# Down projections of an encoder trunk: twelve instead of eight inner chunks by half-block products

## The chip, the cores and the metric

The kernel runs on one core of a Trainium2 chip. The metric is the device time of one execution in microseconds. A core has TensorE (PE in the profile; its weight loads are shown as PEld), VectorE (DVE), ScalarE (ACT), GpSimd (POOL) and SyncE (SP), which run their own instruction queues in order and wait for one another by semaphores. Transfers are issued from the queues of SP and POOL. Matmul results lie in PSUM, everything else in SBUF.

## The reference

The reference is an encoder of two layers on 512 tokens of width 1024 in float32. Each layer has a SwiGLU half step, an attention mixer, a second SwiGLU half step and a gated embedding:

```python
def swiglu(x, w_gate, w_up, w_down):
    return (jax.nn.silu(x @ w_gate) * (x @ w_up)) @ w_down
...
h = h + 0.5 * swiglu(rmsnorm(h, norm_ffn1[i]), ...)
h = h + ab_mixer(...) if i % 2 == 0 else h + c_mixer(...)
h = h + 0.5 * swiglu(rmsnorm(h, norm_ffn2[i]), ...)
h = h + sigmoid(rmsnorm(h, norm_ple[i]) @ w_ple_gate[i]) * (p[i] @ w_ple_proj[i])
```

The inner width is 2816, which is 22 chunks of 128. So there are four down projections, from 22 inner chunks to 8 output chunks of 128 features by 512 tokens.

## The kernel before

Activations lie transposed, features on the partitions and 512 tokens along the row. Float32 accuracy is kept by splitting each operand into a high part (a rounded copy, ScalarE, line 149) and a low part (the difference, VectorE, line 150); a product is three matmuls: high by high, high by low, low by high.

In `ffn` the gate and up projections make the inner chunks one after the other (m = 0 to 21). Each is split into two activation tiles of the pool `act`. The first eight are also stored unsplit to DRAM (`raw`, line 408, from POOL's queue).

`down` (line 418) then makes the output chunks in four pairs. The first pair is plain: for each output 22 chunks of 128, three matmuls of 512 columns each (`plain`, lines 433 to 440), with weights loaded in units of up to eight chunks, and every unit split into a tile of `whi` and one of `wlo` (four buffers each). During that pair `inner_sums` (line 504) fetches the stored chunks k and k + 4 for k = 0 to 3 and makes the combinations that the half-block products need.

For the other three pairs (m = 2, 4, 6), inner chunks 0 to 7 go by seven products instead of eight: two outputs by two groups of four chunks by two halves of the tokens make a two by two block product, and Winograd's form of Strassen's scheme needs seven block products of 256 columns. `inner_weights` (line 521) loads 1024 columns of both outputs and combines them on VectorE (lines 529 to 533), making four weight tiles: wa, wb, ws, wr. The seven products go into PSUM banks p1, p2 (pool `psmm`, three buffers), y (`pss`) and z (`pso`). Then y is copied (lines 482 and 489), combined with z (490 to 492) and added to the residual (494). The remaining 14 chunks of each output are added plainly, into p1 and p2, and `evict` (line 442) adds the bank to the residual, stores the output to `kept` in DRAM and normalises it (`norm_chunk`: lines 199 and 200 make the split, 207 the square, 214 the running sum of squares on POOL). Outputs in LATER (3, 4, 5) are not normalised then; they are fetched back behind the seven products of the last pair (lines 495 to 498) and normalised there. The sum of squares gives the next stage its scale: it is read by small matmuls at line 221.

The framework orders instructions by priority, which is their order in the program, and by when it estimates buffers to be free; it inserts the semaphores. So weights of later pairs, and of the next stage, are loaded and split ahead as far as the buffers (five raw weight tiles `wraw`, four of `whi` and `wlo`) allow. Temporary tiles come from a pool of eight (`tmp`), small weight pieces from two buffers (`rb`).

The four downs are followed by the mixer `ab` (line 744), the embedding `ple`, the mixer `c`, and `ple` again. Each begins with matmuls over the eight normalised chunks in order.

Of the kernel before, what the change touches and what calls it, by code (L numbers as in the profile page):

```python
# [28 lines left out]
UNIT = 8 * P  # L29
# [18 lines left out]
class Trunk:  # L48
# [3 lines left out]
    def __init__(self, ctx, tc, io):  # L52
# [4 lines left out]
        self.sp = pool("small", 2)  # L57
        self.ap_ = pool("act", ACTS)
        self.tp = pool("tmp", TMPS)
# [330 lines left out]
    def ffn(self, i, which, k_next):  # L390


        nc, io = self.nc, self.io
        gu, dn = io[f"gu{which}"], io[f"dn{which}"]
        first = i == 0 and which == 1
        a, y, t = [], [None] * KC, [None] * (KC // 2)

        kept = io["xT"].rearrange("p c t -> c p t") if first else self.put_away()
        raw = self.dp.tile([2 * SEVEN, P, T], F32, name=self.nm("inner"))
        for m in range(NF):  # L400
            if m < FRONT:
                r = self.pair_front(gu[i, m], m, first, gu[i, m + 1])
            elif m in FAST:
                r = self.pair_fast(gu[i, m], y, t)
            else:
                r = self.pair(gu[i, m], y)
            if m < 2 * SEVEN:
                nc.gpsimd.dma_start(raw[m], r)
            ah, al = self.act(F32R), self.act(F32R)
            self.split(r, ah, al)  # L410
            a.append((ah, al))
            for c, after in enumerate(SUMS):
                if m == after:
                    y[c], y[c + KC // 2], t[c] = self.halves(c)
        self.begin_norm(k_next)
        self.down(dn[i], a, raw, kept)

    def down(self, w, a, raw, kept):

        nc, H = self.nc, T // 2
# [3 lines left out]
        later = []  # L426

        def fetched(m, where):
            h = self.tmp()
            nc.sync.dma_start(h, where[m])  # L430
            return h

        def plain(p, m, s, e, start):
            u = self.unit(w[m, :, s * P:e * P], (e - s) * P)
            for j, (xh, xl) in enumerate(a[s:e]):
                c = slice(j * P, (j + 1) * P)
                mm = nc.tensor.matmul
                mm(p, u[0][:, c], xh, start=start and j == 0, stop=False, skip_group_check=True)  # L438
                mm(p, u[0][:, c], xl, start=False, stop=False, skip_group_check=True)  # L439
                mm(p, u[1][:, c], xh, start=False, stop=s + j == NF - 1, skip_group_check=True)  # L440

        def evict(m, p, h):
            stt(h, p, 0.5, h, op0=ALU.mult, op1=ALU.add)
# [17 lines left out]
        for m in range(2, KC, 2):  # L461
            hs = [fetched(m + j, kept) for j in range(2)]
            wa, wb, ws, wr = self.inner_weights(w[m, :, :UNIT], w[m + 1, :, :UNIT])
            M = UNIT // 2
            p1, p2, y, z = self.bank(), self.bank(), self.sbank(), self.obank()
            x11 = [(h[:, l], lo[:, l]) for h, lo in a[:SEVEN]]
            x21, x22 = [[(h[:, c], lo[:, c]) for h, lo in a[SEVEN:2 * SEVEN]] for c in (l, r)]
            t4 = [(h[:, r], lo[:, r]) for h, lo in a[:SEVEN]]
            t1, t2 = [[(h[:, c], lo[:, c]) for h, lo, _ in sums] for c in (l, r)]
            t3 = [(t[:, l], t[:, r]) for _, _, t in sums]  # L470

            def product(out, u, off, xs, start=False, stop=False):
                mm = nc.tensor.matmul
                for k, (xh, xl) in enumerate(xs):
                    c = slice(off + k * P, off + (k + 1) * P)
                    mm(out, u[0][:, c], xh, start=start and k == 0, stop=False, skip_group_check=True)
                    mm(out, u[0][:, c], xl, start=False, stop=False, skip_group_check=True)
                    mm(out, u[1][:, c], xh, start=False, stop=stop and k == SEVEN - 1, skip_group_check=True)

            e, f, u2 = self.tmp(), self.tmp(), self.tmp()  # L480
            product(y[:, l], wa, 0, x11, True)
            act(e[:, l], y[:, l], AF.Copy)
            product(p1[:, l], wa, M, x21, True)
            product(p2[:, l], wb, 0, t4, True)
            product(z[:, l], ws, M, t1, True, True)
            product(y[:, r], ws, 0, t3)
            product(p1[:, r], wr, M, x22)
            product(y[:, l], wr, 0, t2, False, True)
            act(u2[:, l], y[:, l], AF.Copy)
            tt(e[:, r], z[:, l], u2[:, l], op=ALU.add)  # L490
            tt(f[:, l], y[:, r], u2[:, l], op=ALU.add)
            tt(f[:, r], z[:, l], f[:, l], op=ALU.add)
            for h, x in zip(hs, (e, f)):
                stt(h, x, 0.5, h, op0=ALU.mult, op1=ALU.add)
# [4 lines left out]
            for j, p in enumerate((p1, p2)):  # L499
                for s in range(2 * SEVEN, NF, 8):  # L500
                    plain(p, m + j, s, min(NF, s + 8), False)
                evict(m + j, p, hs[j])

    def inner_sums(self, k, a, raw):
# [6 lines left out]
        nc.sync.dma_start(x2, raw[k + SEVEN])  # L511
        s, q = self.tmp(), self.tmp()
        for d, p, m in ((s[:, l], x[:, r], x[:, l]), (s[:, r], x2[:, r], s[:, l]),
                        (q[:, l], x2[:, r], x[:, r]), (q[:, r], x2[:, l], s[:, r])):
            nc.vector.tensor_tensor(d, p, m, op=ALU.subtract)  # L515
        t3 = self.act(F32R)
        self.split(q[:, l], t3[:, l], t3[:, r])
        self.split(q[:, r], a[k][0][:, r], a[k][1][:, r])
        return (*self.split_chunk(s, nc.vector), t3)

    def inner_weights(self, w1, w2):

        nc, M = self.nc, UNIT // 2
        ra, rs = [self.wr.tile([P, UNIT], F32, tag="wr", name=self.nm("wr")) for _ in range(2)]
        nc.sync.dma_start(ra, w1)
        nc.sync.dma_start(rs, w2)
        tt = nc.vector.tensor_tensor
        wa, wb = self.parts(ra), self.parts(rs[:, M:])
        tt(rs[:, M:], rs[:, :M], rs[:, M:], op=ALU.add)
        tt(rs[:, :M], ra[:, :M], rs[:, :M], op=ALU.subtract)  # L530
        ws = self.parts(rs)
        tt(ra[:, :M], rs[:, M:], ra[:, :M], op=ALU.subtract)
        tt(ra[:, M:], ra[:, M:], ra[:, :M], op=ALU.subtract)
        return wa, wb, ws, self.parts(ra)

    def parts(self, raw):
        n = raw.shape[-1]
        hi = self.wh.tile([P, UNIT], F32R, tag="wh", name=self.nm("wh"))
        lo = self.wl.tile([P, UNIT], F32R, tag="wl", name=self.nm("wl"))
        self.split(raw, hi[:, :n], lo[:, :n])  # L540
        return hi, lo

    def put_away(self):

# [880 lines left out]
```

## Time and profile before

| | us |
|---|---|
| Three runs | 2040.48, 2041.50, 2044.54 |
| Profiled execution | 2042.86 |
| Its span (first to last instruction) | 2041.1 |
| TensorE busy | 2019.5 |
| VectorE busy | 1520.3 |
| ScalarE busy | 1056.9 |
| GpSimd busy | 260.2 |

A profile row of a group shows the source line, the engine, the operation, what it writes and reads, shapes, count, busy time and mean duration in ns, then the idle time of the engine before it and what ended that. A timeline row shows start and duration in us, engine, line, operation and tiles, and in brackets the idle time before and its releaser. A row of windows shows for each engine its busy time in the stretch and the number of instructions, then the granted TensorE clock, the share of the transfer engines and GB/s. Durations of matmuls overlap, so their rate is read from start to start. The span is 1.8 us shorter than the profiled execution's time.

### The profile page before, as it was taken

How to read it: one execution, taken by the hardware profiler on the slowest of the kernel's cores; microseconds unless marked ns; L12 is line 12 of the kernel's file. 1: busy time of each engine (PE TensorE's matmuls, PEld its weight loads, DVE VectorE, ACT ScalarE, POOL GpSimd, SP SyncE). 2: the span in 40 equal slices, each digit the busy share in tenths (PEclk: the TensorE clock that was granted, in tenths of full speed). 3: DMA queues.
4: the chain of work that ended last, by engine and by line, in shares of the span. 5: the costliest groups of instructions: out<-in, count | busy, mean ns of one | idle time of the engine just before them, and what ended most of it. 6: DMA issues, size and time to landing. Idle time of an engine off the chain costs nothing.

```text
span 2041.1 us, 33721 instructions
## 1 busy us (share of the span) xinstructions
PE 2019.5 (99%) x12862; PEld 1820.6 (89%) x12862; DVE 1520.3 (74%) x2575; ACT 1056.9 (52%) x1798; POOL 260.2 (13%) x294
## 2 busy tenths in 40 slices
PE   9999999999999999999999999999999999999997
PEld 6999988878888899988888999888888889998886
DVE  7888865598766988875668888756788688888554
ACT  6555533377644555552445555434666545555242
POOL 0100011342212110000211100002000111000021
PEclk9999999999999999999999999999999999999999
DMA  7777644553425576653545775645343447665451
GB/s 212 193 188 188 181 139 157 150 104 73 100 73 165 137 195 182 170 191 124 185 150 159 192 183 158 201 125 161 109 112 102 155 134 192 184 179 165 132 193 42
DMA packets 123123, 312.94 MB, mean 153 GB/s; under 512 B 23504, under 2 KB 31184, under 8 KB 122960
## 3 DMA queue, kind: packets, MB, share of 16 engines
q1 hardware_dynamic: 104064, 253.06, 38.3%
q0 software_dynamic: 18752, 57.69, 15.0%
q8 instruction: 101, 1.65, 0.3%
q14 instruction: 62, 0.51, 0.1%
q10 hardware_dynamic: 144, 0.04, 0.0%
HBM read 274.02 MB, written 25.66 MB: 147 GB/s over the span
## 4 chain that ended last, share of the span: by engine, by line
PE 90%; DVE 3%; DMA 2%; ACT 2%; issue 1%; POOL 1%; SPq 0%; DVEq 0%; POOLq 0%; ACTq 0%
PE mm L362 6%; PE mm L361 6%; PE mm L360 6%; PE mm L174 6%; PE mm L438 6%; PE mm L439 6%; PE mm L173 6%; PE mm L440 6%; PE mm L175 6%; PE sc L362 3%; PE sc L361 3%; PE sc L360 3%; PE sc L175 3%; PE sc L173 3%; PE sc L174 3%; PE ob L360 2%
## 5 line engine op out<-in xcount | busy, mean ns | idle before, releaser
L149 ACT ACTIVATE wh<-wr 128x1024 fp32r<-128x1024 f32 (+2 forms) x455 | 466.2, 1026 | 541.5 <-PE mm L439 170.7
L150 DVE TENSOR_TENSOR wl<-wr,wh 128x1024 fp32r<-128x1024 f32 (+2 forms) x455 | 542.8, 1196 | 203.6 <-ACT wh L149 198.1
L362 PE MATMUL mm<-act,wl 128*128 128x256 f32 x1088 | 307.9, 283 | 0.0
L361 PE MATMUL mm<-act,wh 128*128 128x256 f32 x1088 | 307.9, 283 | 0.0
L360 PE MATMUL mm<-act,wh 128*128 128x256 f32 x1088 | 307.9, 283 | 0.0
L173 PE MATMUL mm<-act,wh 128*128 128x512 f32 (+1 forms) x648 | 254.4, 393 | 0.9 <-ACT act L149 0.4
L174 PE MATMUL mm<-act,wh 128*128 128x512 f32 (+1 forms) x648 | 254.2, 392 | 0.7 <-DVE act L200 0.6
L175 PE MATMUL mm<-act,wl 128*128 128x512 f32 (+1 forms) x648 | 253.3, 391 | 0.0
L361 PEld LDWEIGHTS mm<-act,wh 128*128 128x128 f32 x1088 | 208.9, 192 | 0.4
L362 PEld LDWEIGHTS mm<-act,wl 128*128 128x128 f32 x1088 | 208.9, 192 | 0.2
L360 PEld LDWEIGHTS mm<-act,wh 128*128 128x128 f32 x1088 | 208.9, 192 | 0.2
L438 PE MATMUL mm<-act,wh 128*128 128x512 f32 x512 | 199.4, 389 | 0.0
L439 PE MATMUL mm<-act,wh 128*128 128x512 f32 x512 | 199.4, 389 | 0.0
L440 PE MATMUL mm<-act,wl 128*128 128x512 f32 x512 | 199.2, 389 | 0.0
L149 ACT ACTIVATE act<-tmp 128x512 fp32r<-128x512 f32 (+1 forms) x204 | 113.7, 590 | 83.0 <-DVE tmp L515 33.1
L360 PE MATMUL sc<-act,wh 128*128 128x256 f32 x544 | 154.0, 283 | 0.0
L361 PE MATMUL sc<-act,wh 128*128 128x256 f32 x544 | 154.0, 283 | 0.0
L362 PE MATMUL sc<-act,wl 128*128 128x256 f32 x544 | 154.0, 283 | 0.0
L174 PEld LDWEIGHTS mm<-act,wh 128*128 128x128 f32 x648 | 122.2, 189 | 24.5 <-DVE act L200 2.2
L173 PEld LDWEIGHTS mm<-act,wh 128*128 128x128 f32 x648 | 121.9, 188 | 23.9 <-ACT act L199 0.8
L175 PEld LDWEIGHTS mm<-act,wl 128*128 128x128 f32 x648 | 122.1, 188 | 22.1 <-DVE wl L150 0.2
L150 DVE TENSOR_TENSOR act<-tmp,act 128x512 fp32r<-128x512 f32 (+1 forms) x200 | 125.7, 643 | 9.7 <-ACT act L149 7.7
(224 smaller groups left out, 4430.0 us busy)
## 6 DMA issues: line engine op xcount, KB each, us to landing
wr<-in_gu_dram SPq DMA_DIRECT2D x176, 512.0 KB, 4.7
wr<-in_gu_dram POOLq DMA_DIRECT2D x68, 512.0 KB, 5.5
wr<-in_dn_dram SPq DMA_DIRECT2D x64, 512.0 KB, 3.9
rb<-in_gu_dram SPq DMA_DIRECT2D x68, 256.0 KB, 3.0
wr<-in_dn_dram SPq DMA_DIRECT2D x32, 384.0 KB, 3.2
wr<-in_qk_ab_dram SPq DMA_DIRECT2D x20, 512.0 KB, 3.3
tmp<-kept SPq DMA_DIRECT2D x36, 256.0 KB, 4.1
inner<-tmp POOLq DMA_DIRECT2D x32, 256.0 KB, 3.6
```

What stands on the lines that cost most here:

```text
L149: self.put(self.nc.scalar.activation(hi, src, AF.Copy))
L150: self.put((lo_eng or self.nc.vector).tensor_tensor(lo, src, hi.bitcast(F32), op=ALU.subtract))
L173: mm(out, stat[0], mov[0], start=start, stop=False)
L174: mm(out, stat[0], mov[1], start=False, stop=False)
L175: return mm(out, stat[1], mov[0], start=False, stop=stop)
L360: mm(out, w[0][:, c], xs[k][0][:, x], start=start and k == 0, stop=False, skip_group_check=True)
L361: mm(out, w[0][:, c], xs[k][1][:, x], start=False, stop=False, skip_group_check=True)
L362: mm(out, w[1][:, c], xs[k][0][:, x], start=False, stop=stop and k == half - 1, skip_group_check=True)
L438: mm(p, u[0][:, c], xh, start=start and j == 0, stop=False, skip_group_check=True)
L439: mm(p, u[0][:, c], xl, start=False, stop=False, skip_group_check=True)
L440: mm(p, u[1][:, c], xh, start=False, stop=s + j == NF - 1, skip_group_check=True)
```

## The change

Twelve inner chunks go by seven products. They are paired by the table TWO: chunk k of the first group with its partner in the second. Chunks 0 to 11 are stored to DRAM; six sums are made during the first pair. `inner_weights` loads, beside the 1024 columns, 512 more of both outputs into the two buffers `rb`, and makes six weight tiles instead of four, some of them filled from two sources. A product runs over six chunks. The remaining ten chunks of an output are plain, as two units of five. In the second pair (m = 2) the plain chunks come first and the seven products add to them; in the third and fourth pairs the products come first, as before. LATER holds outputs 1 to 5 instead of 3 to 5. The activation pool has 64 tiles instead of 62.

```diff
-SEVEN = 4
-LATER = 3, 4, 5
+TWO = (0, 4), (1, 5), (2, 6), (3, 7), (8, 10), (9, 11)
+SEVEN = 12
+LATER = 1, 2, 3, 4, 5
-ACTS = 62
+ACTS = 64
...
-            if m < 2 * SEVEN:
+            if m < SEVEN:
                 nc.gpsimd.dma_start(raw[m], r)
...
+        def others(p, m, start, stop):
+            mid = (SEVEN + NF) // 2
+            plain(p, m, SEVEN, mid, start, False)
+            plain(p, m, mid, NF, False, stop)
...
         for s in range(0, NF, 8):
+            e = min(NF, s + 8)
             for m in range(2):
-                plain(ps[m], m, s, min(NF, s + 8), s == 0)
-            if s == 0:
-                sums = [self.inner_sums(k, a, raw) for k in range(SEVEN)]
+                plain(ps[m], m, s, e, s == 0, e == NF)
+            sums += [self.inner_sums(k, k2, a, raw) for k, k2 in TWO if s <= max(k, k2) < e]
...
+        def seven(m, p1, p2, first, hs):
+            a11, a12, a22, s1, s2, s3, s4 = self.inner_weights(w[m], w[m + 1])
+            y, z = self.sbank(), self.obank()
             e, f, u2 = self.tmp(), self.tmp(), self.tmp()
+            product(y[:, l], a11, x11, True)
             act(e[:, l], y[:, l], AF.Copy)
+            product(p1[:, l], a12, x21, first)
+            product(p2[:, l], a22, t4, first, not first)
+            product(z[:, l], s1, t1, True, True)
+            product(y[:, r], s3, t3)
+            product(p1[:, r], s4, x22, False, not first)
+            product(y[:, l], s2, t2, False, True)
             act(u2[:, l], y[:, l], AF.Copy)
...
+        for m in range(2, KC, 2):
+            hs = [fetched(m + j, kept) for j in range(2)]
+            ps = self.bank(), self.bank()
+            first = m > 2
+            if first:
+                seven(m, *ps, True, hs)
             if m == KC - 2:
                 for c in later:
                     self.h[c] = fetched(c, self.kept)
                     self.norm_chunk(c)
+            for j, p in enumerate(ps):
+                others(p, m + j, not first, first)
+                if first:
+                    evict(m + j, p, hs[j])
+            if not first:
+                seven(m, *ps, False, hs)
+                for j, p in enumerate(ps):
+                    evict(m + j, p, hs[j])
...
+        (ga,), (gb, b22) = parts(ra), parts(ra2, rs[:, M:])
         tt(rs[:, M:], rs[:, :M], rs[:, M:], op=ALU.add)
         tt(rs[:, :M], ra[:, :M], rs[:, :M], op=ALU.subtract)
+        (gs,) = parts(rs)
+        hi, lo = tile(self.wh, "wh", F32R), tile(self.wl, "wl", F32R)
+        self.split(rs2[:, G:], hi[:, :G], lo[:, :G])
+        tt(rs2[:, G:], rs2[:, :G], rs2[:, G:], op=ALU.add)
+        tt(rs2[:, :G], ra2[:, :G], rs2[:, :G], op=ALU.subtract)
+        self.split(rs2, hi[:, G:G + M], lo[:, G:G + M])
...
         tt(ra[:, :M], rs[:, M:], ra[:, :M], op=ALU.subtract)
         tt(ra[:, M:], ra[:, M:], ra[:, :M], op=ALU.subtract)
+        (gr,) = parts(ra)
+        tt(ra2[:, :G], rs2[:, G:], ra2[:, :G], op=ALU.subtract)
+        tt(ra2[:, G:], ra2[:, G:], ra2[:, :G], op=ALU.subtract)
+        (gr2,) = parts(ra2)
+        return (ga[:4] + gb[:2], ga[4:] + gb[2:], b22 + d22, gs[4:] + d1, gr[:4] + gr2[:2], gs[:4] + d3,
+                gr[4:] + gr2[2:])
```

More of the change, by code (lines that the diff above doesn't have):

```diff
@@ new lines, in down, with product @@
+        x11 = [tuple(x[:, l] for x in a[k]) for k, _ in TWO]
+        x21, x22 = [[tuple(x[:, c] for x in a[k]) for _, k in TWO] for c in (l, r)]
+        t4 = [tuple(x[:, r] for x in a[k]) for k, _ in TWO]
+        t1, t2 = [[(h[:, c], lo[:, c]) for h, lo, _ in sums] for c in (l, r)]
+        t3 = [(t[:, l], t[:, r]) for _, _, t in sums]
+        def product(out, us, xs, start=False, stop=False):
+            mm = nc.tensor.matmul
+            for k, (u, (xh, xl)) in enumerate(zip(us, xs)):
+                mm(out, u[0], xh, start=start and k == 0, stop=False, skip_group_check=True)
+                mm(out, u[0], xl, start=False, stop=False, skip_group_check=True)
+                mm(out, u[1], xh, start=False, stop=stop and k == len(xs) - 1, skip_group_check=True)
@@ L498, in down, with inner_sums @@
                     self.norm_chunk(c)
[L499 to L504, printed above, removed]
+            for j, p in enumerate(ps):
[6 more added lines that the diff above has]
+                    evict(m + j, p, hs[j])
+    def inner_sums(self, k, k2, a, raw):
         nc, H = self.nc, T // 2
@@ new lines, in inner_weights, with parts @@
+        raws = []
+        for n, s in ((UNIT, 0), (M, UNIT)):
+            for x in (w1, w2):
+                raws.append(tile(self.wr, "wr", F32) if n == UNIT else
+                            self.tp.tile([P, T], F32, tag="rb", name=self.nm("rb"), bufs=2))
+                dma(raws[-1], x[:, s:s + n])
+        ra, rs, ra2, rs2 = raws
+        def parts(*srcs):
+            hi, lo, out, n = tile(self.wh, "wh", F32R), tile(self.wl, "wl", F32R), [], 0
+            for x in srcs:
+                c = slice(n, n + x.shape[-1])
+                self.split(x, hi[:, c], lo[:, c])
+                out.append([(hi[:, i:i + P], lo[:, i:i + P]) for i in range(c.start, c.stop, P)])
+                n = c.stop
+            return out
```

52 lines of the change are left out of this document (9 added, 43 removed).

## The prediction

> **What bounds the kernel now.** I read the page first (busy time, the clock row, the chain that ended last), then the windows of the four down projections, then the timeline of TensorE at the borders of output pairs.
>
> ```profile
> PE 2019.5 (99%) x12862; PEld 1820.6 (89%) x12862; DVE 1520.3 (74%) x2575; ACT 1056.9 (52%) x1798; POOL 260.2 (13%) x294
> PEclk9999999999999999999999999999999999999999
> PE 90%; DVE 3%; DMA 2%; ACT 2%; issue 1%; POOL 1%; SPq 0%; DVEq 0%; POOLq 0%; ACTq 0%
> ```
> ```profile
> core 0: us, PE busy (x) PEld busy (x) DVE busy (x) ACT busy (x) POOL busy (x), PEclk, DMA share, GB/s
> 239.60:357.20 117.60, 117.60 (x639) 102.55 (x639) 75.69 (x104) 45.49 (x66) 13.78 (x13) 1.00 0.51 163
> ...
> 1852.40:1969.90 117.50, 117.50 (x639) 102.45 (x638) 75.29 (x104) 45.37 (x66) 14.30 (x13) 1.00 0.49 163
> ```
> ```profile
> 239.66 0.40 PE L438 MATMUL mm<-act,wh 128*128 128x512 f32 x1
> ...
> 269.61 0.28 PE L476 MATMUL sc<-act,wh 128*128 128x256 f32 x1
> ...
> 279.68 0.40 PE L438 MATMUL mm<-act,wh 128*128 128x512 f32 x1
> ...
> 298.75 0.28 PE L476 MATMUL sc<-act,wh 128*128 128x256 f32 x1
> ```
>
> The chain is 90% TensorE at the full clock, and in a down projection TensorE never rests. Start to start is what counts, since matmuls overlap: the first pair has 22 x 2 x 3 = 132 matmuls of 512 columns from 239.66 to 269.61, 226.9 ns each. The second has 84 of 256 columns (seven products of four chunks by three) in 10.07 us, 119.9 ns each, and 84 of 512 in 19.07 us, 227.0 ns each. Nothing is left over for a wait. A half-width matmul costs 53% of a full one, which is what the change must live with.
>
> **TensorE's part.** In each of three pairs per down, seven products of six chunks (126 matmuls of 256) take the place of seven of four (84), and 20 plain chunk-outputs (60 of 512) that of 28 (84). That is +42 x 119.9 - 24 x 227.0 = 5036 - 5448 = -412 ns a pair, in twelve pairs -4.95 us, 0.24%. No more can come from it, so every microsecond of stall counts. A pair is then 15.1 us of products and 13.6 us of plain work, where it was 10.1 and 19.1.
>
> The Trainium skill, "TensorE: Matmul & The Clock Gate", section "Wait — 56ns, not 53.3ns?", gives N / 2.4 GHz plus about 2.5 ns from start to start, 109.2 and 215.8 ns. By that a pair would save 593 ns, 7.1 us in all, and the time would be an estimated 2034.4. The rows do not agree (13 and 11 ns a matmul in place of 2.5), and the rows decide.
>
> **The work beside it.**
>
> ```profile
> L150 DVE TENSOR_TENSOR wl<-wr,wh 128x1024 fp32r<-128x1024 f32 x406 | 501.4, 1237 | 184.5 <-ACT wh L149 179.0 <-PE mm L477 2.0 <-PE sc L175 1.7
> L150 DVE TENSOR_TENSOR wl<-wr,wh 128x768 fp32r<-128x768 f32 x32 | 30.6, 957 | 17.2 <-ACT wh L149 17.1
> L150 DVE TENSOR_TENSOR wl<-rb,wh 128x512 fp32r<-128x512 f32 x68 | 46.9, 690 | 4.7
> L150 DVE TENSOR_TENSOR act<-tmp,act 128x256 fp32r<-128x256 f32 x32 | 13.4, 420 | 1.2 <-ACT act L149 0.2
> L515 DVE TENSOR_TENSOR tmp<-tmp,tmp 128x256 f32<-128x256 f32 x48 | 18.2, 421 | 1.6 <-DMA tmp<-inner 1.4
> L408 POOL DMA_DIRECT2D inner<-tmp x32 | 20.7, 646 | 153.8 <-DVE tmp L387 86.8 <-DVE tmp L304 33.6 <-DVE tmp L284 33.3
> L360 PE MATMUL mm<-act,wh 128*128 128x256 f32 x1088 | 307.9, 283 | 0.0
> ```
>
> Weights, per pair on VectorE: three more 512-column splits (3 x 0.69), one of 256 (0.42), four more combinations of 256 (4 x 0.42), and for the plain chunks four splits of 640 columns (no row; between 0.69 and 0.96, taken at the middle, 0.82) in place of two of 1024 and two of 768 (4.39). Net +3.1 us. Sums: two more per down, each four subtractions, two 256 splits and one 512 split, 4 x 0.42 + 2 x 0.42 + 0.69 = 3.2 us. A down gains 3 x 3.1 + 2 x 3.2 = 15.6 us of VectorE: 75.7 becomes 91 of 116, 79%. ScalarE makes one copy for each split and no combination, so it grows by less than that: under 61 of 116, from 45.5. On the average all of it hides behind TensorE; what matters is where it falls due.
>
> SP issues twelve more transfers per down: two 256 KB weight pieces a pair, four reads for the sums, two refetches of outputs. POOL issues four more stores of inner chunks during the gate and up pairs. Three of a down's eight stores fall into such half-block pairs now, and TensorE's products there (L360) have no idle before them, so I cost the new ones at nothing; uncovered each would be its issue, 0.65 us (L408). The two extra activation tiles and the DMA bytes (the windows show a share of 0.5) cost nothing by themselves.
>
> **First pair.** Six sums instead of four.
>
> ```profile
> 239.60:269.60 30.00, 30.00 (x134) 24.85 (x134) 24.45 (x45) 12.97 (x23) 0.58 (x1) 1.00 0.54 180
> 298.70:327.80 29.10, 29.10 (x169) 25.81 (x169) 15.09 (x19) 8.29 (x10) 1.10 (x2) 1.00 0.43 137
> ```
>
> VectorE goes from 24.5 to some 31 us in 30, so the sums run into the second pair. There they are first needed by the third product (the right halves of the first operands). With the plain chunks first that is 13.6 + 4.3 us into the pair; the overrun of 1 to 3 us is covered. Without that reordering it would not be.
>
> **Second to third pair.** Here the change makes a new wait. The second pair ends with products and the third begins with them: twelve weight tiles in a row through four buffers, and the second pair's two evictions come only after its last product. There are three PSUM buffers for outputs, so the third pair's third product (a22, into p2) needs the first of these evictions, 2 x 2.16 = 4.3 us after the border.
>
> ```profile
> 280.51 0.37 ACT L489 ACTIVATE tmp<-sc 128x256 f32<-128x256 f32 x1
> 281.52 0.42 DVE L490 TENSOR_TENSOR tmp<-ob,tmp 128x256 f32<-128x256 f32 x1
> 283.24 0.69 DVE L494 SCALAR_TENSOR_TENSOR tmp<-tmp,tmp 128x512 f32<-128x512 f32 x1
> 357.23 0.69 DVE L443 SCALAR_TENSOR_TENSOR tmp<-mm,tmp 128x512 f32<-128x512 f32 x1 [1.12 <-PE mm L440]
> ```
>
> From the copy of the last product to the last of the five combining operations is 280.51 to 283.93, 3.4 us; with 0.2 before (357.03 to 357.23 is what an eviction now waits for the last matmul) and an eviction of 0.7 (L443) behind, 4.3: exactly due. Behind it on VectorE wait the third pair's s1 and a22 splits; if one of 1.24 us is queued ahead, a22 waits about that long. Bounds 0 to 1.7 us a down; I take 0.3, near the lower end, because 2.4 us of the 3.4 are work and the rest waiting for a split that ScalarE ran first.
>
> **The end of each down.** Five outputs (1 to 5) instead of three are fetched back and normalised behind the last products, and the plain stretch that covers this shrinks from 19.1 to 13.6 us.
>
> ```profile
> 340.33 1.30 SPq L430 DMA_DIRECT2D tmp<-kept  x2
> 346.13 0.43 SPq L430 DMA_DIRECT2D tmp<-kept  x1
> 345.90 0.72 ACT L199 ACTIVATE act<-tmp,gain 128x512 fp32r<-128x512 f32 x1 [1.44 <-DMA tmp<-kept]
> 346.66 0.75 DVE L200 SCALAR_TENSOR_TENSOR act<-tmp,gain,act 128x512 fp32r<-128x512 f32 x1 [0.94 <-ACT act L199]
> 349.73 4.15 DVE L200 SCALAR_TENSOR_TENSOR act<-tmp,gain,act 128x512 fp32r<-128x512 f32 x3
> 354.02 2.10 DVE L150 TENSOR_TENSOR wl<-wr,wh 128x1024 fp32r<-128x1024 f32 x1
> 349.84 5.19 POOL L214 TENSOR_TENSOR ssq<-ssq,tmp 128x512 f32<-128x512 f32 x3 [0.58 <-ACT tmp L207]
> 357.03 0.39 PE L173 MATMUL sc<-act,wh 128*128 128x512 f32 x1
> 359.24 0.75 DVE L200 SCALAR_TENSOR_TENSOR act<-tmp,gain,act 128x512 fp32r<-128x512 f32 x1
> ```
> ```profile
> 338.00:357.00 19.00, 19.00 (x86) 15.73 (x85) 13.29 (x14) 9.07 (x13) 6.89 (x5) 1.00 0.52 171
> ```
>
> The products end at 357.03 - 19.07 = 337.96. Now the first refetch is used 7.9 us after that, and chunk 6's low part (the last of the three) is done at 353.9, 3.1 us before the next stage begins at 357.03. That stage reads chunk c after c x 3 x 227 ns, so chunk 6 is due at 361.3 (slack 7.4) and chunk 7, done at 360.0, is due at 362.0 (slack 2.0). The change takes 5.4 us off the stretch. Two more chunks cost 0.75 us each alone, but beside POOL's squares the same operation takes 1.7 (three in 4.15, the first alone): +1.5 to +3.4 us. Together 6.9 to 8.8 against 7.4: chunk 6 is between 0.5 early and 1.4 late, and chunk 7's eviction and split stand behind it. By the window: 13.3 us of VectorE plus 2 x 1.7 less 0.5 for smaller plain splits (0.82 twice for 0.96 and 1.23) is 16.2 in 13.6, and the excess of 2.6 must fit in the 4.8 us before chunk 7 is due, together with the wait for the first refetch. So lateness is 0 to 2.6 us a down. I take 0.7, nearer to nothing, since chunk 6 comes out about even.
>
> The Trainium skill, "SBUF — State Buffer", section "Who interferes with whom", says that a VectorE instruction with two SBUF inputs and a GpSimd one that reads SBUF shut each other out for the whole instruction; 0.75 against 1.7 us agrees. It speaks against the change: the two more squares and splits run one behind the other.
>
> ```profile
> 1399.44 0.69 DVE L214 TENSOR_TENSOR ssq<-ssq,tmp 128x512 f32<-128x512 f32 x1
> 1400.19 0.26 PE L221 MATMUL tr<-ones,ssq 128*128 128x1 f32 x1
> 1001.67 0.50 PE L174 MATMUL sc<-act,wh 128*128 128x512 f32 x1 [0.22 <-POOL act L150]
> ```
>
> Behind the third down the sum of squares ends at 1400.13 and TensorE reads it at 1400.19: no slack. Behind the second (and fourth) TensorE already idles a little for POOL's split of p, which hides part of a late chunk.
>
> **Sum.** -4.95 + 4 x 0.3 + 4 x 0.7 = -0.95 us. The profiled execution took 2042.9 (span 2041.1 and 1.8 around it), so 2041.9; the median of three runs is 1.4 less, 2041.5, and the forecast goes by it: **2040.5**. A measurement of this kernel can tell about 0.2%, 4.1 us, from no change.
>
> **The rivals.**
> Forecast (0.45): savings mostly given back at the borders, own range 2037.5 to 2045.5.
> Everything hides (0.28): border and end cost nothing, 2041.5 - 4.95 = 2036.6. For it: four downs of 117.5 us without one TensorE gap now, and VectorE idle for a fifth even afterwards. Against: the 1400.13 to 1400.19 row and the even reckoning of chunk 6.
> Late outputs at the end (0.20), the case on the slow side: refetches four and five queue on SP behind weight loads that wait for a buffer (as the third at 346.13 came 5.8 us after the first), chunks 5 to 7 come 2.6 us late each time: -4.95 + 1.2 + 4 x 2.6 = +6.6, 2048.1. It is slower by 0.2% from 2.0 us a down on. For it: the rows above. Against: the next stage asks for chunk 5 only 3.4 us after it begins.
> The PSUM wait between second and third pair (0.07): at 1.7 a down, -4.95 + 4 x (1.7 + 0.7) = +4.7, 2046.2. For it: 4.3 due, 4.3 needed. Against: the scheduler may put the eviction ahead of the splits.
>
> That the products are not made at all cannot be, the counts are written out.
>
> **How the numbers follow.** Faster by 0.2% needs nearly all of the saving: 0.28. Slower are both last rivals, less a little of the milder one that stays under 4.1: 0.25. Within: 0.47. The range takes the hidden case with 0.8 below it (a shorter wait for p than now), and reaches to the late case: 2035.8 to 2048.5, leaving some 0.17 out.
>
> **What would show it.** A down's TensorE window of 116.1 us instead of 117.5 if the sum holds; idle before a22 of the third pair, released by the eviction, if the PSUM wait is real; idle at the first matmuls behind a down, released by L199's or L200's successors, if the outputs are late; the refetch issues on SP within 4 us of one another if they are not. I am wrong if VectorE's queue order differs from the program's there, since a single 1.2 us split at either place is a fourth of the saving.

## The result and the profile after

The change makes the kernel **slower by 11.4 us**: a median of 2053.49 us (2051.70 to 2054.57, six runs) against 2042.04 (2040.48 to 2044.54, six runs), a ratio of 1.0055 with a 95% interval of 1.0044 to 1.0066. The profiled execution took 2051.70, the fastest of the six, with a span of 2049.7, so the traces account for 8.6 us of span. The other five executions had a mean granted clock of 0.994 to 0.996 where the profiled one had 0.997, so they spent more time at a lower clock; in which places, no trace shows. One execution of the kernel before, run beside e9 to e11 below, took 4005.9 us and counts in none of the ratios.

From the page of the kernel after, the span and the busy line:

```profile
span 2049.7 us, 34578 instructions
PE 2017.0 (98%) x13078; PEld 1827.1 (89%) x13078; DVE 1567.6 (76%) x2727; ACT 1079.3 (53%) x1870; POOL 268.8 (13%) x310
```

TensorE is busy 2.5 us less in a span 8.6 us longer: what is new is idle time. The windows of the first and the last down of the kernel after:

```profile
239.10:355.60 116.50, 116.50 (x693) 104.19 (x692) 83.66 (x138) 47.28 (x78) 7.81 (x10) 1.00 0.53 176
1858.80:1975.20 116.40, 116.40 (x694) 104.09 (x693) 82.06 (x138) 47.61 (x78) 8.09 (x10) 1.00 0.53 171
```

A down, from the start of its first matmul to that of the next stage's first, takes 116.29 us where it took 117.37: -1.08 each, -4.3 in all. The loss stands behind the downs. In the table, idle is the time by which two neighbouring TensorE starts lie further apart than usual for their width (0.06, 0.12 or 0.23 us), counted from an excess of 0.06 us on, in the 25 us behind a down.

| idle behind a down, us | 1st | 2nd | 3rd | 4th | sum |
|---|---|---|---|---|---|
| before | 0.17 | 1.03 | 0.17 | 1.90 | 3.3 |
| after | 1.47 | 3.44 | 5.99 | 5.26 | 16.2 |

12.9 us more idle less 4.3 saved is the 8.6 us of span. The worst place is the third down, which ends at 1397.18. The timeline of SP in the kernel after, with starts, durations and what is issued (L430 fetches an output back, L167 loads weights):

```profile
1384.95 0.38 SPq L430 DMA_DIRECT2D tmp<-kept  x1
1385.43 1.26 SPq L167 DMA_DIRECT2D wr<-in_qk_c_dram  x1
1386.79 0.38 SPq L430 DMA_DIRECT2D tmp<-kept  x1
1389.30 0.33 SPq L167 DMA_DIRECT2D wr<-in_qk_c_dram  x1
1389.72 0.38 SPq L430 DMA_DIRECT2D tmp<-kept  x1
1394.31 0.33 SPq L167 DMA_DIRECT2D wr<-in_qk_c_dram  x1
1394.73 0.51 SPq L430 DMA_DIRECT2D tmp<-kept  x1
1397.15 0.33 SPq L167 DMA_DIRECT2D wr<-in_qk_c_dram  x1
1397.53 0.42 SPq L430 DMA_DIRECT2D tmp<-kept  x1
```

Each of the last four fetches leaves right behind a weight load, and the fifth is issued after the down has ended. The chain of waits from there (start, duration, what):

```profile
1395.91 1.22 DVE wl L151
...
1397.15 0.33 SPq L167
...
1397.53 3.90 DMA tmp<-kept
...
1402.08 0.62 ACT tmp L208
...
1402.84 1.30 POOL ssq L215
...
1404.20 1.61 POOL ssq L215
1405.81 4.86 issue
1410.71 1.96 POOL rcol L225
```

Read from the top: a split ends at 1397.13 and frees a raw weight buffer; the load that waited for that buffer goes; the fetch behind it in the queue goes 0.4 us later and takes 3.90 us to land; only then are the chunk's high part, its square and the last sums on POOL made. What TensorE makes of the late chunks (timeline, then a window of the same stretch, in which the figure behind POOL's is the granted clock):

```profile
1399.90 0.39 PE L174 MATMUL mm<-act,wh 128*128 128x512 f32 x1
1402.29 0.50 PE L175 MATMUL mm<-act,wh 128*128 128x512 f32 x1 [2.00 <-DVE act L201]
...
1403.93 0.63 PE L175 MATMUL mm<-act,wh 128*128 128x512 f32 x1
1404.36 0.63 PE L176 MATMUL mm<-act,wl 128*128 128x512 f32 x1
...
1410.61 0.40 PE L176 MATMUL mm<-act,wl 128*128 128x512 f32 x1
1412.72 0.65 PE L241 MATMUL tr<-ident,rcol 128*128 128x128 f32 x4 [1.72 <-POOL rcol L225]
```
```profile
1403.50:1406.90 3.40, 3.40 (x9) 2.61 (x9) 3.40 (x3) 1.46 (x3) 2.23 (x2) 0.51 0.53 154
```

The wait that ends at 1402.29 is for the chunk of the fourth fetch, not of the fifth: the stage reads the chunks in order, three matmuls each, and the one at 1399.90 is the first of chunk 4. That fetch was issued at 1394.73 and landed at 1398.73. Then VectorE still had a weight split to do, and the chunk's low part took 1.74 us beside a sum on POOL (VectorE's timeline):

```profile
1399.36 1.21 DVE L151 TENSOR_TENSOR wl<-wr,wh 128x1024 fp32r<-128x1024 f32 x1
1400.49 1.74 DVE L201 SCALAR_TENSOR_TENSOR act<-tmp,gain,act 128x512 fp32r<-128x512 f32 x1
```

The fifth chunk's low part is ready in time; it is paid for later, through the sum of squares. Late chunks are thus paid three times: 2.27 us of waiting for a chunk, 1.56 us because for 3.4 us after it the clock is granted at 0.51 (matmuls of 512 columns start 0.43 us apart instead of 0.23), and 2.16 us around the reciprocal root. The last sum, on VectorE, ends at 1406.97, and TensorE reads it at 1409.48, behind matmuls of the same stage; only two of these (1410.29 and 1410.61) are left to run while the root is made, where the kernel before had eight (1401.10 to 1403.02). Together the three are the 5.99 of the table.

### The profile page after: what moved, and what is told of

Same layout as the page of the kernel before. It is cut to its first block, busy times and chain, and to the rows that moved or that the text cites. A ratio compares the mean times of both kernels' runs of the same rounds, so it can differ in the third digit from the quotient of the medians.

```text
span 2049.7 us, 34578 instructions
## 1 busy us (share of the span) xinstructions
PE 2017.0 (98%) x13078; PEld 1827.1 (89%) x13078; DVE 1567.6 (76%) x2727; ACT 1079.3 (53%) x1870; POOL 268.8 (13%) x310
## 4 chain that ended last, share of the span: by engine, by line
PE 72%; DVE 3%; ACT 2%; issue 2%; DMA 1%; POOL 1%; SPq 0%; DVEq 0%; POOLq 0%; ACTq 0%
PE mm L175 5%; PE mm L174 5%; PE mm L176 5%; PE mm L363 5%; PE mm L362 5%; PE mm L361 5%; PE mm L439 3%; PE mm L438 3%; PE mm L440 3%; PE sc L363 2%; PE sc L362 2%; PE sc L361 2%; PE sc L175 2%; PE sc L176 2%; PE sc L174 2%
## 5 line engine op out<-in xcount | busy, mean ns | idle before, releaser
L150 ACT ACTIVATE wh<-wr 128x1024 fp32r<-128x1024 f32 (+3 forms) x455 | 454.8, 1003 | 437.6 <-DVE wr L351 83.6
L151 DVE TENSOR_TENSOR wl<-wr,wh 128x1024 fp32r<-128x1024 f32 (+3 forms) x455 | 526.8, 1163 | 161.7 <-ACT wh L150 140.6
L150 ACT ACTIVATE act<-tmp 128x512 fp32r<-128x512 f32 (+1 forms) x228 | 123.6, 578 | 108.8 <-DVE tmp L530 54.6
L438 PE MATMUL mm<-act,wh 128*128 128x512 f32 x416 | 162.0, 389 | 0.0
L439 PE MATMUL mm<-act,wh 128*128 128x512 f32 x416 | 162.0, 389 | 0.0
L440 PE MATMUL mm<-act,wl 128*128 128x512 f32 x416 | 161.8, 389 | 0.0
L151 DVE TENSOR_TENSOR act<-tmp,act 128x512 fp32r<-128x512 f32 (+1 forms) x224 | 137.3, 630 | 11.1 <-ACT act L150 7.4
```

The costliest lines, as they stand in the source:

```text
L150: self.put(self.nc.scalar.activation(hi, src, AF.Copy))
L151: self.put((lo_eng or self.nc.vector).tensor_tensor(lo, src, hi.bitcast(F32), op=ALU.subtract))
L440: mm(p, u[1][:, c], xh, start=False, stop=stop and j == e - s - 1, skip_group_check=True)
```

## The experiments

Theory A: the five fetches come too late, by their place in SP's queue. Rivals: POOL's sums of squares hold VectorE back; five chunks are too many for a cover of 13.6 us, whenever they come; the new pairs themselves stall. Ratios are against the kernel before, run beside each (its medians were 2041.4 to 2042.1, so medians of different rows are comparable to about 0.7 us). Idle is that of the profiled execution.

| run | median us (runs) | ratio, 95% interval | span | idle behind downs 1 to 4 |
|---|---|---|---|---|
| e1 after, fetches into act | 2042.99 (11) | 1.0008 [0.9999, 1.0017] | 2038.6 | 0.17 2.52 0.43 3.15 |
| e2 after, squares on VectorE | 2047.46 (9) | 1.0024 [1.0015, 1.0034] | 2044.2 | 0.34 3.83 3.23 3.90 |
| e3 before, LATER 1 to 5 | 2055.14 (4) | 1.0062 [1.0048, 1.0075] | 2053.6 | 1.21 3.87 6.21 4.96 |
| e4 after, fetches by POOL | 2060.69 (4) | 1.0088 [1.0073, 1.0104] | 2059.5 | 3.72 6.63 8.65 6.01 |
| e5 = e3 + fetches into act | 2040.99 (10) | 0.9994 [0.9985, 1.0003] | 2039.2 | 0.17 0.56 0.17 0.54 |
| e6 = e1, products first | 2046.47 (10) | 1.0020 [1.0011, 1.0029] | 2046.4 | 0.17 6.46 0.42 4.14 |
| e7 = e1 + early p | 2044.65 (11) | 1.0013 [1.0004, 1.0022] | 2039.6 | 0.17 3.27 0.18 3.02 |
| e8 before, fetches into act, early p | 2041.24 (11) | 0.9996 [0.9987, 1.0005] | 2039.4 | 0.17 0.56 0.18 0.55 |
| e9 = e1, norm in the products | 2054.69 (4) | 1.0060 [1.0043, 1.0077] | 2055.3 | 0.17 3.63 0.25 1.32 |
| e10 = e7 + squares on VectorE | 2037.89 (10) | 0.9981 [0.9972, 0.9990] | 2035.2 | 0.17 0.81 0.48 1.52 |
| e11 = e9 + early p, VectorE | 2037.91 (11) | 0.9982 [0.9973, 0.9991] | 2035.9 | 0.17 0.55 0.25 0.55 |
| e12 = e1 + squares on VectorE | 2041.03 (10) | 0.9993 [0.9983, 1.0002] | 2040.0 | 0.17 3.97 0.18 1.45 |

**e1, fetches into act tiles**

```diff
-        def fetched(m, where):
-            h = self.tmp()
+        def fetched(m, where, new=self.tmp):
+            h = new()
...
-                    self.h[c] = fetched(c, self.kept)
+                    self.h[c] = fetched(c, self.kept, self.act)
+                for c in later:
                     self.norm_chunk(c)
```

> The changed kernel, but the five later outputs are fetched back into activation tiles (free once the last pair's first operands are read) instead of the eight temporary ones, and all five fetches stand ahead of the first normalisation in the program. Theory A (the refetches come late, behind weight loads that wait for a raw buffer on SP and behind full temporary tiles): all five issued before the products of the last pair end, TensorE idle in the first 20 us behind a down back from 1.5, 3.4, 6.0 and 5.3 us to about 0.1, 1, 0.2 and 1.9, time 2037 to 2039. Theory B (VectorE's splits and POOL's squares do not fit into 13.6 us of plain work, whenever the data come): idle shrinks by less than a third, time 2048 or more.

The 11.4 us shrink to 0.9. SP's timeline in e1, at the same down:

```profile
1369.97 2.23 SPq L430 DMA_DIRECT2D act<-kept  x5
```

All five leave in one go, 10 us before the products end (the down ends at 1393.96, and its last 60 plain matmuls take 13.6). Theory A holds for the first and third down; 2.5 and 3.2 us are left behind the other two, and the median is 4 us above the theory's range. Behind those two TensorE waits for the split of `p`, the second input of the stage `ple` (TensorE's timeline in e1):

```profile
998.85 0.50 PE L175 MATMUL sc<-act,wh 128*128 128x512 f32 x1 [0.84 <-POOL act L151]
```

The second chunk of p lands at 998.05 and 1972.59, 6.2 and 6.3 us after the ends of the second and the fourth down.

**e2, sums of squares behind a down on VectorE instead of POOL**

```diff
-            eng = nc.vector if c == KC - 1 or self.k == 0 else nc.gpsimd
+            eng = nc.vector if c == KC - 1 or self.k in (0, 1, 3, 5, 7) else nc.gpsimd
```

> The changed kernel, with the sums of squares behind the downs on VectorE instead of POOL, so nothing shuts VectorE out; refetches as they are. Theory A: the last refetch is still issued about when the down ends, the time falls by 0 to 4 us (the additions behind it are shorter), 2049 to 2053. Theory B: the splits take 0.75 us each again, most of the idle goes, 2040 to 2045.

It lies between both. POOL has a part of 6.0 us in the loss while the fetches are still late (behind the third down the fifth is issued at 1395.42, and the down ends at 1395.37), but it isn't the whole.

**e3, the kernel before with LATER = 1, 2, 3, 4, 5 and nothing else**

> The kernel before, with LATER = 1 to 5 alone: eight chunks by products, 19.1 us of plain work behind the last products. Theory A: refetches four and five stand behind the same waiting weight loads on SP, so most of the loss is there without the shorter stretch, 5 to 12 us slower than before, 2047 to 2054. Theory B: 19.1 us hold the two more chunks nearly, 0 to 3 us slower than before.

This one line costs 13.1 us without any product changed, a little more than theory A had. Its SP timeline shows the same picture as that of the kernel after: the fifth fetch is issued 1.3 us before its down ends (1399.6), behind a weight load:

```profile
1397.87 0.33 SPq L166 DMA_DIRECT2D wr<-in_qk_c_dram  x1
1398.29 0.38 SPq L430 DMA_DIRECT2D tmp<-kept  x1
```

**e4, the five fetches issued from POOL's queue** (`nc.gpsimd.dma_start` in place of `nc.sync.dma_start` for them)

> The changed kernel, with the five refetches issued from POOL's queue, still into temporary tiles. If SP's waiting weight loads alone delay them (theory A1), they are issued within 3 us of the products' end and the time falls to 2038 to 2043. If the temporary tiles do (theory A2), or if POOL's in-order queue puts each behind a square that waits for the one before, the third to fifth stay late and the time is 2048 to 2056.

Worse than either range. POOL also runs in order, and behind the third down its timeline has the last fetch queued after a sum of squares:

```profile
1399.28 1.79 POOL L215 TENSOR_TENSOR ssq<-ssq,tmp 128x512 f32<-128x512 f32 x1
1401.02 0.56 POOL L430 DMA_DIRECT2D tmp<-kept  x1
```

So another queue alone is no remedy. In e1 the kind of tile, the order in the program (all fetches ahead of the first norm_chunk) and the place in the queue change together, as the framework orders by its estimate of when a tile is free. In the kernel after, the fifth fetch followed its weight load without a wait of its own, which speaks for the queue; that the tmp tiles are why it was put there is argued, not shown.

**e5, e3 with the fetches of e1**

> The kernel before with LATER = 1, 2, 3, 4, 5 and, as in e1, the five chunks fetched again into tiles of act, all fetches ahead of the first norm_chunk. Nothing is left out. Theory A (what LATER = 1..5 costs, 13 us in e3, is the lateness of the fetches that wait for tmp tiles): about the time of before, 2041 to 2044, TensorE idle in the 25 us behind the four downs together under 6.5 us (e1: 6.3; before: 3.1; e3: 16.3). Rival (five chunks are too many to square, sum and split at a down's end, whenever their data come): 2048 to 2055, idle 10 us or more. e1 has a shorter cover than this kernel (36 instead of 56 plain products' matmuls beyond the sevens in a pair), so if A holds and the cover matters, this one shows less idle time than e1.

14 us come back, and the idle time is the least of all (1.4 us in sum; e8 and e11 come within 0.1 of it). So five chunks are not too many for the old cover of 19.1 us. The covers to compare are 84 plain matmuls here and 60 in e1, not the 56 and 36 of the expectation. With the new cover of 13.6 us (e1) the idle sum is 6.3 instead of 1.4 us: the new pairs cost 4.8 us behind the downs, more than the 4.3 that the products save. Here the second chunk of p lands only 3.3 and 3.5 us after the ends of the second and the fourth down (997.68 and 1972.59), where in e1 it was 6.2 and 6.3. The rival is right in that the shorter cover does not hold the work.

**e6, e1 with the products first in the second pair too** (`first = True`)

> e1 with the products ahead of the plain chunks in the second pair too (first = True). Nothing is left out. Theory that the order matters (in e1 VectorE ends the last sums of inner chunks at 272.7 and the split of the first product weights at 275.8, 2.5 us after the last eviction of the first pair starts at 273.3): TensorE stands 1 to 4 us at the start of each second pair, 2047 to 2059. Rival (without the two 640-column splits in front of them, the weights of the products are split as early as those of the plain chunks are in e1): under 0.5 us in each down, 2042 to 2045.

The order matters, but less than the theory had it: the median is 3.5 us above e1's and lies between the two ranges. The four downs take 118.16, 116.47, 117.49 and 116.17 us, 3.1 more than in e1 together, nearly all of it in the first and the third. The 6.46 us behind the second down hold 6.8 us at a granted clock of 0.50 (1003.5 to 1010.3), and the profiled execution is the slowest of the ten, so this figure is not typical. The stall in the first down is not at the first product but at the fourth, and waits for weights. TensorE's timeline in e6:

```profile
276.90 0.28 PE L476 MATMUL ob<-act,wh 128*128 128x256 f32 x1
278.46 0.38 PE L477 MATMUL ob<-act,wl 128*128 128x256 f32 x1 [1.27 <-DVE wl L151]
```

**e7 and e8, p loaded and split in the down, with early fetches: after and before**

```diff
+                if self.p_of is not None:
+                    self.p = []
+                    for c in range(2):
+                        raw = self.act()
+                        nc.sync.dma_start(raw, self.io["pT"][self.p_of, :, c, :])
+                        self.p.append(self.split_chunk(raw))
```

> e1, and the two chunks of p for the stage ple that follows the down of FFN2 are loaded into act tiles and split right behind the five fetches, in down itself, instead of at the start of ple. Nothing is left out. Theory: what is left in e1 behind the second and fourth down (TensorE idle 2.52 and 3.15 us, before 1.03 and 1.90) is the load of p, issued behind a weight load that waits for a buffer; with p early both fall to about 0.5 us: 4.7 us off e1's 2043.0, so 2037 to 2040. Rival (the idle time there is the chain of squares and sums on POOL, or the splits of p now in front of norm chunks on ACT and VectorE delay them as much): 2041.5 to 2045.

> The kernel before (four chunk pairs, LATER = 3, 4, 5) with both edits of e7: fetches into act tiles ahead of the norm chunks, p loaded and split in down. Nothing is left out. It says what the four times 1.08 us of shorter products (twelve chunk pairs in six sums instead of eight in four) are worth when both kernels have the same end of a down: if the saving stands, this kernel is 4 us slower than e7; if the better cover of the longer plain part gives it back, within 1.5 us of e7. Against before itself: idle behind the second and fourth down 1.03 and 1.90 us, so at most 2 to 2.5 us off, 2039.5 to 2042.

e7's theory fails, and the rival's range holds: nothing is gained over e1, and the wait has only moved from p to a norm chunk. The timeline of TensorE in e7 behind the second down:

```profile
998.46 0.50 PE L174 MATMUL mm<-act,wh 128*128 128x512 f32 x1 [1.39 <-ACT act L200]
999.50 0.50 PE L175 MATMUL mm<-act,wh 128*128 128x512 f32 x1 [0.54 <-DVE act L201]
```

e8, the same end on the longer cover, has no such waits. In span the two are equal (2039.6 and 2039.4 us), in the median e8 is 3.4 us faster: the better cover gives back the saving and more.

**e9, e1 with the five fetches and norm chunks between the third and the fourth product**

```diff
             product(p2[:, l], a22, t4, first, not first)
+            mid()
```

> e1 with the five fetches and their norm_chunks put between the third and the fourth of the last pair's seven products, where the act tiles of a11's and a22's inner chunks come free, instead of behind the seventh: four products of 18 matmuls of 119.9 ns, 8.6 us, more of cover. Nothing is left out. Theory (what e1 has left behind the second and fourth down, 2.5 and 3.2 us where e5 has 0.6 and 0.5, is a cover shorter by 24 matmuls of 227 ns, 5.4 us, in which VectorE runs five L201 of 1.3 to 1.8 us beside the squares' sums on POOL and so splits the next stage's weights late): idle behind the four downs 0.2 to 0.6 each as in e5, 4.3 us under e5, 2035 to 2038. Rival (the fetches and norm chunks now stand in front of the last evictions and of the weight splits and wait for act tiles in order, so that TensorE waits inside the down): down windows over 117 us, 2043 or more.

The rival came true: 11.7 us slower than e1, now inside the downs (120.75, 120.67, 120.45 and 119.93 us, each with one stretch of 3.4 us at a granted clock of 0.50). VectorE's timeline in e9, then TensorE's:

```profile
335.12 8.07 DVE L201 SCALAR_TENSOR_TENSOR act<-act,gain,act 128x512 fp32r<-128x512 f32 x5 [2.21 <-ACT act L200]
343.12 3.02 DVE L151 TENSOR_TENSOR wl<-wr,wh 128x640 fp32r<-128x640 f32 x4
```
```profile
341.02 0.40 PE L439 MATMUL mm<-act,wh 128*128 128x512 f32 x1
343.99 0.50 PE L440 MATMUL mm<-act,wl 128*128 128x512 f32 x1 [2.57 <-DVE wl L151]
```

Five low parts hold VectorE for 8.07 us, 1.6 each, and the plain chunks' weight splits stand behind them in order.

**e10, e7 with the sums of squares on VectorE**

> e7 with the sums of squares of the chunks behind a down on VectorE instead of POOL, as in e2. Nothing is left out. In e7 a chunk costs VectorE 1.78 us (L201 beside a POOL sum) behind the second down, against 0.74 + 0.68 = 1.42 us here: for five chunks 1.8 us less in front of the splits of the next stage's weights. Theory of the shorter cover with VectorE as its bound: idle behind the second and fourth down 3.3 and 3.0 falls to 0.5 to 2.0 each, 2039.5 to 2043. Rival (VectorE alone now carries the sums that POOL carried beside it): no gain, 2044 to 2047.

Better than expected, **faster than both kernels**: 2037.89, 0.9981 [0.9972, 0.9990] of before. The groups of VectorE by form from 979 to 997, first in e7, then in e10 (count, busy us and mean ns):

```profile
L201 DVE SCALAR_TENSOR_TENSOR act<-act,gain,act 128x512 fp32r<-128x512 f32 x5 | 8.2, 1679 | 0.5 <-ACT act L200 0.5
```
```profile
L215 DVE TENSOR_TENSOR ssq<-ssq,tmp 128x512 f32<-128x512 f32 x7 | 4.7, 678 | 0.0
L201 DVE SCALAR_TENSOR_TENSOR act<-act,gain,act 128x512 fp32r<-128x512 f32 x5 | 3.7, 739 | 0.0
```

Five low parts hold VectorE for 8.2 us beside POOL's sums; in e10 the five and seven sums together take 3.7 + 4.7 = 8.4, and no sum is left to come. What follows on VectorE is earlier: the last chunk's low part, in the timelines of e7 and e10:

```profile
998.70 0.74 DVE L201 SCALAR_TENSOR_TENSOR act<-tmp,gain,act 128x512 fp32r<-128x512 f32 x1
```
```profile
995.18 0.74 DVE L201 SCALAR_TENSOR_TENSOR act<-tmp,gain,act 128x512 fp32r<-128x512 f32 x1
```

with downs that end within 0.1 us of one another (991.90 and 991.84). The two totals of 8.2 and 8.4 us are equal, so they alone don't make the 3.5 us. In e7 other work of VectorE is longer too beside POOL's sums (an addition of 0.68 us takes 1.79, a split of 1.21 takes 1.71), and one weight split more stands ahead of the last eviction, which starts at 996.97 instead of 993.45. The edit moves only the sums; how much each of these brings, the runs don't part.

**e11, e9 with both edits of e10**

> e9 with the early p of e7 and the sums of squares on VectorE of e10. Nothing is left out. If each takes something off what is left behind the downs, idle 0.2 to 0.6 behind each down and no half rate, 2034 to 2037, below both kernels; if the place of the fetches alone decides, the same as e9 within 1.5 us; if the norm work inside the products delays the last pair, 2041 or more.

The same as e10, just above the range for a gain. With low parts of 0.74 us the place inside the products does little harm: the downs take 1.0 us more together (116.76, 116.47, 116.57 and 116.27), against 1.5 us less idle time behind them.

**e12, e1 with the sums on VectorE, p loaded late**

> e1 (five fetches into act tiles, ahead of the norm chunks) with the sums of squares behind the downs on VectorE as in e2 and e10; p is loaded in ple, as in the kernel after. Nothing is left out. It parts the two edits of e10 over e1. If VectorE's stretched L201 beside POOL is all that e1 has left: as e10, span 2035 to 2036.5, median 2037 to 2039, idle behind the second and fourth down under 1.6 us each. If the late load of p is a wait of its own that e7 only hid behind the late splits: idle of 1.5 to 3 us behind the second and fourth down, median 2039.5 to 2043.

It parts e10's two edits. Behind the fourth down the sums alone are enough (1.45): p's second chunk lands 4.4 us after the down's end. Behind the second, 3.97 us are left. About 1.7 of them (an estimate: half of its 3.4 us) are a stretch at half the clock, which e1's trace does not have:

```profile
1002.60:1006.00 3.40, 3.40 (x12) 2.81 (x12) 0.16 (x1) 0.00 (x0) 1.04 (x1) 0.50 0.43 154
```

The rest is about what e1 had there, and the chain of waits is that of p, as in e1:

```profile
991.06 1.24 DVE wl L151
...
992.31 0.33 SPq L167
...
993.17 6.28 DMA tmp<-in_pT_dram
...
1001.50 0.50 PE sc L175
```

The load of p waits in SP's queue behind a weight load that waits for a split, as the fetches did; the second chunk lands at 999.45, 6.1 us after the down's end (993.39). So e10 needs both edits: with the sums moved alone, p stays late behind the second down; with p early alone (e7), VectorE is late. The gain of e12 over e1, 2.0 us, is not clear of noise (the intervals of the two ratios overlap); e10's is.

## Why the prediction was wrong, step by step

**The saving** was right: -412 ns for each of twelve pairs, -4.95 us. Measured are -4.3, in which the border's idle time is contained: 4 x (1.08 + 0.15) = 4.9. The forecast of 116.1 us for a down stands against 116.29; it leaves out the 0.3 us of the border that the sum takes. One reading beside the sum is off: "13 and 11 ns a matmul" takes 106.7 from 119.9 but 215.8 from 227.0, once without and once with the formula's 2.5 ns. Taken alike they are 13.2 and 13.7. Nothing else in the prediction uses them.

**The work beside it** was sized too high: VectorE was to gain 15.6 us a down; on the page it gains 1567.6 - 1520.3 = 47.3 us, 11.8 a down, and in the first down's window it reaches 83.7 us where 91 was forecast. The single prices hold (a split of 640 columns takes 821 ns, 0.82 was taken). But the prediction added whole durations, and on VectorE these overlap: a split that starts at 299.24 lasts 1.22 us, and the next instruction starts at 300.37. The POOL stores put at nothing cost nothing that can be seen: the stages between the downs grow by the idle time behind them within 0.5 us.

**The first pair** was right that plain-first covers the overrun. What it covers was named wrongly: e6 shows the fourth product waiting for the split of its weights (278.46), where the prediction had the sums. The price of the other order is 3.1 us in the four downs of e6's profiled execution.

**Second to third pair**: a real wait, 0.15 us a down where 0.3 was taken (bounds 0 to 1.7), at another place. The timelines of TensorE and VectorE in the kernel after:

```profile
302.00 0.28 PE L477 MATMUL mm<-act,wl 128*128 128x256 f32 x1
302.20 0.36 PE L475 MATMUL ob<-act,wh 128*128 128x256 f32 x1
```
```profile
301.63 0.42 DVE L495 TENSOR_TENSOR tmp<-ob,tmp 128x256 f32<-128x256 f32 x1
301.97 0.68 DVE L448 SCALAR_TENSOR_TENSOR tmp<-mm,tmp 128x512 f32<-128x512 f32 x1
```

The framework ran s1 (into `ob`) ahead of a22, so by the times the wait is for the last reading of `ob`, until 302.05, not for an eviction (the row names no releaser). That the size came near is luck.

**The end of each down is the step that failed.** "So lateness is 0 to 2.6 us a down. I take 0.7, nearer to nothing". Measured, the idle time grew by 1.30, 2.41, 5.82 and 3.36 us, 3.2 on average and in two of four above the bound. The step counted VectorE's work in the 13.6 us and the wait for the first refetch, 7.9 us, as it stood; it took all five to come as the three had come. The issue times show instead that each fetch further back stands behind another weight load that waits for a buffer, so that the fifth comes 12.6 us after the first (1384.95 to 1397.53) and behind the end of the down. The rival "late outputs at the end" had exactly this mechanism; it had 0.20 and a price of 2.6 us a down. Two things were missing from that price, and the third down shows both: the half clock after the gap (1.6 us) and the late reciprocal root (2.2 us). The low part that takes 1.7 us beside a sum on POOL, which the prediction did price, adds to the lateness of the fourth chunk; e2 puts POOL's part at 6.0 us of the 11.4 while the fetches are late, and e1 takes away 10.5 by the fetches alone, so the parts do not add.

Behind the late fetches lay a second layer, which the prediction had seen as a size and not as a limit: with early fetches the shorter cover still costs 4.8 us against e5, which takes the whole saving. In e1 itself the wait left over is that for p, which the prediction saw ("TensorE already idles a little for POOL's split of p") but gave no growth. With p early (e7) it is VectorE's: a low part takes 1.68 us beside POOL's sums and 0.74 without (e7 and e10), which is the price the prediction used (1.7). The rule that the prediction cited there from the Trainium skill, "SBUF — State Buffer", section "Who interferes with whom", agrees with these two numbers. And e10 with both waits away gets the saving at last: 2037.9 against 2041.2 for e8, the old products with the same early fetches and p, 4.2 us in span. The old products with the sums on VectorE as well were not run; with 1.5 us of idle time left behind e8's downs they could gain little there.

The forecast's median base and the profiled execution's differ by 1.4 us, which changes nothing here. e1 and e7 scatter more (2040.7 to 2049.4 and 2041.4 to 2046.7) than before does (2040.5 to 2044.9 in these runs), and the scatter goes with the mean granted clock of an execution: e1's five up to 2042.9 had 0.997 to 0.998, its three above 2045 had 0.995. A stretch of 3.4 us at half the clock takes 0.0008 off that mean, so the difference would be three or four such stretches, by estimate. Where they lie is open: the profiled executions of e1 and e7 were the fastest of theirs.

## What to carry to other kernels

When a change moves more transfers behind a point in an in-order queue, price the last of them, not the first: look at which waiting load stands ahead of each, for a load that waits for a buffer holds all that follows. A saving on the busiest engine that comes from a shorter stretch also shortens the cover of what ran beside that stretch; move the cover's work first (here fetches and p early, sums on the engine that they would hold back anyway), then shorten. And test repairs in pairs: over e1, early p gained nothing alone and the sums on VectorE 2.0 us (not clear of noise), both together 5.1.

## What the runs showed of the hardware

A gap of 2.39 us between two matmul starts, 2.00 of them idle, was followed by 3.4 us at a granted clock of 0.51, starting 1.2 us after TensorE had begun again; in e9 the same follows a wait of 2.57 us:

```profile
345.50:348.90 3.40, 3.40 (x10) 2.66 (x9) 2.93 (x6) 0.65 (x1) 0.00 (x0) 0.50 0.94 328
```

In e12 it followed two waits of only 0.19 and 0.85 us (until 999.41 and 1001.50; half rate from 1002.6). Yet waits of 1.39 and 0.54 us close to one another (e7) were not followed by it, nor was one of 1.73 us behind the second down of the kernel after (until 1006.52; the granted clock is 1.00 from there to 1014). So the length of a wait alone does not decide, and what does is open. The clock's steps lie on a fixed grid: in e9's trace it falls to half at 345.51, 987.21, 1011.10, 1393.40 and 1970.25 us, which is 188, 7, 112 and 169 times 3.413 us from one to the next.

The Trainium skill, "TensorE: Matmul & The Clock Gate", section "What's actually happening", gives a window of about 3.4 us for the gate, half rate after an idle one: the length agrees with the 3.4 us of the three runs, but an idle time of 2.0 us was enough here, and less in e12.
